# Weight sums, row finishing, output operands and the pool's silu laid at fixed places in a one-core encoder layer

## The chip, the core and the metric

The kernel runs on one core of one Trainium2 chip. The metric is the device time of one execution in microseconds, from the first instruction to the last; lower is better. Five engines matter here: TensorE (PE, matmul), VectorE (DVE), ScalarE (ACT), GpSimd (POOL, nearly idle) and SyncE (SP), which issues almost every DMA.

## The reference

One bidirectional encoder layer, in float32, for 1024 tokens of width 2048:

```python
mod = jax.nn.silu(c) @ w_ada + b_ada
shift, scale, gate = jnp.split(mod, 3, axis=-1)
h = rmsnorm(x, pre_g) * (1.0 + scale[:, None]) + shift[:, None]
proj = h @ w_in
q, k, v, gate_a, u, gate_p = jnp.split(proj, SPLIT_POINTS, axis=-1)
y_a = windowed_gqa(q, k, v, rel_table, sink) * jax.nn.silu(gate_a)
y_p = multiscale_pool(u, w_pool_grp, pool_scale) * jax.nn.silu(gate_p)
g = jax.nn.sigmoid(h @ w_merge + b_merge)
g_a, g_p = jnp.split(g, N_BRANCHES, axis=-1)
merged = g_a * (y_a @ w_br_attn) + g_p * (y_p @ w_br_pool)
o = merged @ w_out
return x + gate[:, None] * rmsnorm(o, post_g)
```

w_in is 2048 x 4608, w_merge 2048 x 4096, w_out 2048 x 2048, the two branch weights 1024 x 2048, w_ada 2048 x 6144. The pool groups average over windows of 2, 4, 8 and 16 tokens.

## The kernel before, in words

**Products.** Every float32 product is made of three matmuls in a rounded float32 form. `split` (L90) takes a tile apart: ACT copies it to the rounded form (hi), DVE subtracts that from the source (lo). PE then adds hi·hi, lo·hi and hi·lo. The large products use a scheme of seven products in place of eight for each 2 x 2 blocks (Strassen and Winograd): `strassen` (L203) makes one "pair" of 256 output columns from seven products of 12 matmuls, each 128x512. The seven need sums of operand blocks (T1 to T4, made once) and of weight blocks (S1 to S4). PE's results lie in three PSUM tiles, X, V and Z; ACT copies them or DVE adds them to earlier parts (u, p, c).

**First pass.** A ramp turns x and makes the first four pairs. `pass1` then runs the pairs 4 to 25, and hands out small steps between products: 36 steps for the modulation (weigh, L458, adds one row of w_ada times silu(c) to `acc` on DVE; sum_columns, L414, adds over partitions with the matmuls PM; mod_columns, L420, writes modc), 32 `gate_step`s (L646, the same for the gate, in `gacc`), the gate's columns, and the 16 `weight_sums` (L617). A weight sum loads four 128x512 blocks of w_out (tag "sw"), makes S1 to S4 in four DVE operations and stores them to DRAM (ws_dS1 to ws_dS4), for the output stage. Its three parts are fetch, make and keep. Before the change they lie from the first step on, evenly over the 22 pairs, and DVE's share of them is placed by the scheduler.

The pairs 26 to 33 run beside the second half of x: fetch_x (L721) loads a tile into the ring `xin` (four buffers), turn_x (L728) transposes it on PE, then modulate and `pre` (L748) prepare operands. Attention follows, then the pool: for each of eight row blocks `window` and `mix` make a window sum, a grouped product and a silu of a loaded gate (tile `sil`, L951).

**Output stage.** The branch products give m in pieces, through DRAM (m_d). `merged_sums` makes operand sums of m (t and B12). `out_pair` (L1145) runs four times, over two halves of the tokens and two of the columns, (0,0), (0,1), (1,0), (1,1); each has seven products of 48 matmuls (`out_mm`, L1110: eight weight blocks, two PSUM tiles, three matmuls). Weights come from w_out or from the stored sums through a ring `wr` of four tiles (512 KB each, two weight blocks) and are split into whi and wlo, four buffers each. `put_step` (L1076) makes one moving operand (mh, ml) out of m, for all four parts at once, after a product, by the hooks after_00 to after_11 (L1279 to L1307).

Rows of o are multiplied by the post norm's weights and squared for the norm. When all four column blocks of a row block are known, `finish_block` (L1132) makes x + o·scale in one DVE operation and stores it. `first_rows` (L1255) does this for the first half's rows during the second half: it loads o from o_d where it isn't kept, and x (tiles `mo`, a ring), two row blocks ahead of the finishing.

**What sets the order.** A tile scheduler places each engine's instructions by priorities and needs, and adds the waits. An instruction that is marked with keep_in_program_order isn't moved: it comes directly behind the instruction that the program wrote ahead of it on the same engine. Each engine, and SP's queue of DMA issues, works in order.

Of the kernel before, what the change touches and what calls it, by code (L numbers as in the profile page):

```python
# [20 lines left out]
P = 128  # L21
# [21 lines left out]
def encoder_layer(ctx: ExitStack, tc: tile.TileContext, x, c, table, w_ada, b_ada, pre_g,  # L43
# [46 lines left out]
    def split(hi, lo, src):  # L90
        nc.scalar.activation(hi, src, AF.Copy)  # L91
        nc.vector.tensor_tensor(lo, src, f32(hi), ALU.subtract)  # L92

    def add(o, a, b, eng=None):
        (eng or nc.vector).tensor_tensor(o, a, b, ALU.add)  # L95

    def sub(o, a, b):
        nc.vector.tensor_tensor(o, a, b, ALU.subtract)
# [488 lines left out]
    wsp = ev_ctx.enter_context(pool("wsum", 6, side="right"))  # L587
# [29 lines left out]
    def weight_sums(j, i):  # L617
# [18 lines left out]
        def keep():  # L636
            for name, t in done:
                store(ws_rows(name)[:, j, i * 512:(i + 1) * 512], t)

        return fetch, make, keep  # L640
# [66 lines left out]
    assert len(steps) == 48 and max(steps) < 7 * n1  # L707
    pass1(n1, side, EASY, steps)
# [39 lines left out]
    def pre(j):  # L748
        t2[j] = pre_op(j, h1, h2, lambda: sp.tile([P, 512], F32, tag="tf", name=uid("tf"), bufs=4))

    side.extend(lambda j=j: pre(j) for j in range(4))
    pass1(PAIRS - i, side, ((0, 1, 2, 4, 5, 6),))
    assert not side
# [154 lines left out]
    with pool("pool") as pp:  # L908
# [30 lines left out]
        def mix(g, j):  # L939
# [9 lines left out]
            sg = pp.tile([P, S], F32, tag="sil", name=f"sil{i}")  # L949
            load(sg, proj_d[COL_GP + i * P:COL_GP + (i + 1) * P, :])  # L950
            nc.scalar.activation(sg, sg, AF.Silu)  # L951
# [11 lines left out]
            store(yp_d[i * P:(i + 1) * P, :], sg)  # L963

        for g, w in enumerate(POOLS):
# [35 lines left out]
    for b, w in enumerate((w_ba, w_bp)):  # L1001
# [4 lines left out]
        else:  # L1006
# [69 lines left out]
    def put_step(n, op, m, t2):  # L1076

        name = MOVING[n]
        for jp in range(JP):
            b11, b12, b21, b22 = (m[kh][jp][:, :, c * 256:(c + 1) * 256] for kh in range(2) for c in range(2))  # L1080
            src = {"B11": b11, "T3": b11, "T2": t2[jp], "B21": b21, "T4": b21, "T1": b12, "B22": b22}[name]
            hi, lo = slot("mh", F32R, (P, 2, 256)), slot("ml", F32R, (P, 2, 256))
            if m is mt and n == 0 and jp == JP - 1:
                tc.keep_in_program_order(nc.scalar.activation(hi, src, AF.Copy))
                sub(lo, src, f32(hi))
            else:
                split(hi, lo, src)
            op[name][jp] = hi, lo
            if name == "B11":
                sub(b11, t2[jp], b11)  # L1090
            elif name == "B21":
                sub(b21, b21, t2[jp])
# [39 lines left out]
    def finish_block(T, n, scale):  # L1132
        r = held.pop((T, n))
        nc.vector.scalar_tensor_tensor(r, r, scale, xrow.pop((T, n)), op0=ALU.mult, op1=ALU.add)
# [10 lines left out]
    def out_pair(half, i, op, after):  # L1145

        final = half == 1 and i == 1
        keep = half == 1 or i == 1
# [15 lines left out]
        def product(wname, mov, pbs, fresh=False):  # L1164

            ws = split_weights(wname)
            nj = 2 * JP
            for j in range(nj - 2):
                w = next(ws)
                for t in range(2):  # L1170
                    out_mm(pbs[t], op, mov, j, t, w, fresh and j == 0, False)
            w = list(ws)
            for t in range(2):
                for j in (nj - 2, nj - 1):
                    out_mm(pbs[t], op, mov, j, t, w[j - nj + 2], False, j == nj - 1)

# [9 lines left out]
        def result(blk, t, src, dst):  # L1186
# [5 lines left out]
            if keep:  # L1192
# [13 lines left out]
        after(0)  # L1206
        product("S3", "T3", bv, True)
        p7 = copies(kept("p7"), bv)
        after(1)
        product("S2", "T2", bz)  # L1210
        u2 = copies(kept("u2"), bz)
        after(2)
# [4 lines left out]
        after(3)  # L1217
# [4 lines left out]
        after(4)  # L1222
# [6 lines left out]
        after(5)  # L1229
        if not final:  # L1230
# [4 lines left out]
            after(6)  # L1235
            return
        c12 = [slot("c12", F32) for _ in range(2)]
# [9 lines left out]
    put_step(0, ops[0], mt, mt2)  # L1247
    put_step(1, ops[0], mt, mt2)
# [30 lines left out]
    def after_00(n):  # L1279
        if n < 5:  # L1280
            put_step(n + 2, ops[0], mt, mt2)
        if n == 6:
            nextm.extend(merged_tiles())
            fetch_merged(nextm, 0)

    def after_01(n):
        if n == 0:
            fetch_merged(nextm, 1)
        if n == 1:
            for jp in range(JP):  # L1290
                merged_sums(nextm, nextt2, jp)
        for step in ((), (), (0,), (1, 2), (3, 4), (5,), (6,))[n]:
            put_step(step, ops[1], nextm, nextt2)

    def after_10(n):
        if n == 0:
            for _ in range(4):
                ring.extend(row_tiles())
# [61 lines left out]
```

## Time and profile before

| what | value |
|---|---|
| median of 3 runs | 2161.96 us (2157.30, 2161.96, 2163.28) |
| profiled execution | 2163.38 us |
| its span in the profile | 2161.6 us |
| mean granted clock of PE | 0.996 |
| DVE's busy time, 150 to 450 us | 226.47 us |
| last stall of PE (Z, first matmul of the last product) | 2141.88 us, 2.64 us |

The profile comes from one execution. The page gives busy times and slices, `--waits`-like lists give for each engine and line what it waited for, and the timeline gives single instructions with their start, their duration and, in brackets, the idle time ahead of them and who ended it. The time between span and device time, 1.8 us, lies around the program. "SPq" is the issue of a DMA, which is not its transfer. The main stages start at about 100 us (first pass), 850 (attention), 1180 (pool), 1517 (branch products) and 1826 (output stage).

### The profile page before, as it was taken

Reading aid. Unit: us, or ns where it says so; the run is one execution under the profiler, and the core shown is the slowest. Engines: PE = TensorE matmul, PEld = TensorE weight load, DVE = VectorE, ACT = ScalarE, POOL = GpSimd, SP = SyncE. Lnnn points to the kernel's source line nnn. Section 1 sums busy time; section 2 is a strip of 40 time slices with the busy share of each in tenths; the row PEclk is TensorE's granted clock in tenths of the full one; section 3 lists DMA queues with packets and bytes.
Section 4 is the critical chain, followed back from the end, with each engine's and each line's share of the span. In section 5 each row is a group of like instructions: output and inputs, shape, how many; then the busy total and the mean of one; then the engine's idle time right before and its main releaser. Section 6 shows DMA issues by size and latency. Waiting matters only on the chain.

```text
span 2161.6 us, 28949 instructions
## 1 busy us (share of the span) xinstructions
PE 2101.6 (97%) x9567; PEld 1716.7 (79%) x9567; DVE 1535.7 (71%) x2754; ACT 1129.2 (52%) x2124; POOL 7.5 (0%) x66
## 2 busy tenths in 40 slices
PE   6999999999999999999999999999999999999997
PEld 3587878888888888888888878888788887878776
DVE  5787777776436676777776878656867878878656
ACT  5653434444374546767775433334645544767554
POOL 0000000000000000000000000000000000000000
PEclk9999999999999999999999999999999999999999
DMA  9888899975443355445445756755654754776986
GB/s 329 287 278 293 293 307 307 323 244 161 151 144 115 117 172 196 164 155 197 155 152 177 250 183 208 245 178 180 221 175 156 239 169 159 264 257 213 301 299 213
DMA packets 303255, 466.11 MB, mean 216 GB/s; under 512 B 23882, under 2 KB 144866, under 8 KB 303104
## 3 DMA queue, kind: packets, MB, share of 16 engines
q1 hardware_dynamic: 301648, 462.02, 65.2%
q0 software_dynamic: 1120, 2.19, 0.3%
q8 instruction: 75, 1.23, 0.2%
q14 instruction: 76, 0.62, 0.1%
q10 hardware_dynamic: 336, 0.06, 0.0%
HBM read 340.41 MB, written 125.85 MB: 216 GB/s over the span
## 4 chain that ended last, share of the span: by engine, by line
PE 75%; DMA 10%; DVE 9%; issue 2%; ACT 2%; SPq 1%; DVEq 0%; ACTq 0%; POOLq 0%
PE Z L228 25%; PE V L228 16%; PE X L228 16%; DVE wlo L92 2%; PE Z L1115 1%; PE Z L1113 1%; PE Z L1114 1%; DMA mo<-in_x_dram 1%; DMA sw<-in_w_out_dram 1%; PE X L1115 1%; PE V L1115 1%; PE V L1113 1%; PE V L1114 1%; PE X L1113 1%; PE X L1114 1%
## 5 line engine op out<-in xcount | busy, mean ns | idle before, releaser
L91 ACT ACTIVATE whi<-raw 128x512 fp32r<-128x512 f32 (+1 forms) x528 | 320.5, 610 | 500.5 <-PE Z L228 256.7
L92 DVE TENSOR_TENSOR wlo<-raw,whi 128x512 fp32r<-128x512 f32 (+1 forms) x528 | 346.6, 662 | 161.4 <-PE Z L228 112.2
L91 ACT ACTIVATE whi<-wr 128x512 fp32r<-128x512 f32 x224 | 138.7, 628 | 92.9 <-DVE wlo L92 30.4
L92 DVE TENSOR_TENSOR wlo<-wr,whi 128x512 fp32r<-128x512 f32 x224 | 149.4, 688 | 43.2 <-ACT whi L91 41.0
L95 DVE TENSOR_TENSOR raw<-raw,raw 128x512 f32<-128x512 f32 x80 | 55.1, 689 | 83.5 <-DMA raw<-in_w_merge_dram 58.5
L1035 ACT ACTIVATE gt<-gt,cols 128x512 f32<-128x512 f32 x64 | 46.0, 723 | 97.9 <-DMA gt<-proj_d 82.1
L228 PE MATMUL V<-T3h,whi 128*128 128x512 f32 x336 | 92.1, 393 | 2.9 <-DVE u L95 2.9
L228 PE MATMUL Z<-B22h,whi 128*128 128x512 f32 x336 | 93.6, 398 | 1.2 <-ACT u L283 1.2
L228 PE MATMUL Z<-T1h,whi 128*128 128x512 f32 x336 | 92.0, 392 | 2.7 <-ACT u L238 1.8
L228 PE MATMUL X<-B11h,whi 128*128 128x512 f32 x336 | 92.5, 393 | 2.1 <-ACT B11h L91 0.8
L228 PE MATMUL V<-T4h,whi 128*128 128x512 f32 x336 | 92.2, 393 | 0.0
L228 PE MATMUL Z<-B22l,whi 128*128 128x512 f32 x336 | 92.1, 394 | 0.0
L228 PE MATMUL Z<-T2h,whi 128*128 128x512 f32 x336 | 91.5, 392 | 0.0
L228 PE MATMUL X<-B11l,whi 128*128 128x512 f32 x336 | 91.3, 390 | 0.2 <-DVE B11l L92 0.2
L228 PE MATMUL Z<-B22h,wlo 128*128 128x512 f32 x336 | 91.3, 392 | 0.0
L228 PE MATMUL Z<-T1l,whi 128*128 128x512 f32 x336 | 91.0, 390 | 0.2 <-DVE T1l L92 0.2
L228 PE MATMUL V<-T3h,wlo 128*128 128x512 f32 x336 | 91.1, 391 | 0.0
L228 PE MATMUL V<-T3l,whi 128*128 128x512 f32 x336 | 91.0, 390 | 0.0
L228 PE MATMUL X<-B21h,whi 128*128 128x512 f32 x336 | 90.9, 390 | 0.0
L228 PE MATMUL V<-T4l,whi 128*128 128x512 f32 x336 | 90.9, 390 | 0.0
L228 PE MATMUL V<-T4h,wlo 128*128 128x512 f32 x336 | 90.8, 389 | 0.0
L228 PE MATMUL Z<-T1h,wlo 128*128 128x512 f32 x336 | 90.7, 390 | 0.0
(308 smaller groups left out, 4851.2 us busy)
## 6 DMA issues: line engine op xcount, KB each, us to landing
part<-part_d SPq DMA_DIRECT2D x136, 256.0 KB, 5.1
ada<-in_w_ada_dram SPq DMA_DIRECT2D x128, 256.0 KB, 5.8
raw<-in_w_in_dram SPq DMA_DIRECT2D x64, 512.0 KB, 4.3
raw<-in_w_merge_dram SPq DMA_DIRECT2D x64, 512.0 KB, 5.3
wr<-ws_dS SPq DMA_DIRECT2D x64, 512.0 KB, 5.1
wr<-in_w_out_dram SPq DMA_DIRECT2D x48, 512.0 KB, 5.3
proj_d<-part SPq DMA_DIRECT2D x68, 256.0 KB, 2.2
sw<-in_w_out_dram SPq DMA_DIRECT2D x64, 256.0 KB, 5.8
```

What stands on the lines that cost most here:

```text
L91: nc.scalar.activation(hi, src, AF.Copy)
L92: nc.vector.tensor_tensor(lo, src, f32(hi), ALU.subtract)
L95: (eng or nc.vector).tensor_tensor(o, a, b, ALU.add)
L228: nc.tensor.matmul(ps, w_[:, i], op[mov][j][m_], start=fresh and i == 0 and n == 0, stop=i == nj - 1 and n == 2, skip_group_check=True)
L1035: nc.scalar.activation(gt, gt, AF.Sigmoid, bias=cols[:, col:col + 1])
L1113: nc.tensor.matmul(pb, hi, w[0], start=first, stop=False, skip_group_check=True)
L1114: nc.tensor.matmul(pb, lo, w[0], start=False, stop=False, skip_group_check=True)
L1115: nc.tensor.matmul(pb, hi, w[1], start=False, stop=last, skip_group_check=True)
```

## The change

1. The weight sums. The four DVE operations of a sum are pinned. Eleven sums are laid from step 70 of the first pass on, behind the 36 modulation steps (which end with about step 70) and among the gate steps; five lie in the pairs 26 to 33, one per pair. They have six buffers in the first part (wsum1) and five in the second (wsum2, also used by `pre`); to make room `xin` has three buffers in place of four.
2. The pool. The gate tile `sil` is loaded one mix ahead, and the silu is pinned on ACT.
3. Operands. `put_step` becomes `put_op(n, jp)`, one part at a time. hi, lo and the follow-up sums of m are pinned, as are both operations of merged_sums. They are laid behind every second weight block of a product (`between`), no longer after it; in the first out_pair each operand is made during the product before the one that uses it.
4. Row finishing. The operation of `finish_block` is pinned, and a step of `first_rows` comes twice per product.

No computation changes, and the number of instructions on each engine stays.

```diff
-            at = [(at, step) for at, step in ((at, steps.get(7 * k + at)) for at in range(7)) if step]
+            at = [(at, step) for at in range(7) for step in steps.get(7 * k + at, ())]
...
-            sub(a["21"], a["11"], a["21"])
-            sub(s2, a["22"], a["21"])
-            add(a["11"], a["11"], s2)
-            sub(a["12"], a["12"], s2)
+            keep(sub(a["21"], a["11"], a["21"]))
+            keep(sub(s2, a["22"], a["21"]))
+            keep(add(a["11"], a["11"], s2))
+            keep(sub(a["12"], a["12"], s2))
...
-    steps = {}
-    for n, three in enumerate(weight_sums(j, h_) for h_ in range(2) for j in range(KT // 2)):
-        for at, step in zip((0, 5, 7), three):
-            steps[7 * n1 * n // 16 + at] = step
-    pass1(n1, side, EASY, steps)
+    def lay_out(n, first, last):
+        steps = {}
+        for k in range(n):
+            for at, step in zip((0, 5, 7), sums.popleft()):
+                steps.setdefault(first + (last - first) * k // n + at, []).append(step)
+        return steps
+    pass1(n1, side, EASY, lay_out(11, 70, 7 * n1 - 2))
...
-    xin = ev_ctx.enter_context(pool("xin", 4, side="right"))
+    xin = ev_ctx.enter_context(pool("xin", 3, side="right"))
+    wsp = mid.enter_context(pool("wsum2", 5))
...
-    pass1(PAIRS - i, side, ((0, 1, 2, 4, 5, 6),))
+    pass1(PAIRS - i, side, ((0, 1, 2, 4, 5, 6),), lay_out(5, 0, 35))
...
-            load(sg, proj_d[COL_GP + i * P:COL_GP + (i + 1) * P, :])
-            nc.scalar.activation(sg, sg, AF.Silu)
+            sg = sils.pop()
+            keep(nc.scalar.activation(sg, sg, AF.Silu))
...
+            if i < NH - 1:
+                fetch_gate_of(i + 1)
...
-                sub(b12, b12, m[0][jp][:, :, 0:256])
+                keep(sub(b12, b12, m[0][jp][:, :, 0:256]))
-                sub(t2[jp], m[1][jp][:, :, 256:512], b12)
+                keep(sub(t2[jp], m[1][jp][:, :, 256:512], b12))
...
-        nc.vector.scalar_tensor_tensor(r, r, scale, xrow.pop((T, n)), op0=ALU.mult, op1=ALU.add)
+        keep(nc.vector.scalar_tensor_tensor(r, r, scale, xrow.pop((T, n)), op0=ALU.mult, op1=ALU.add))
...
                     out_mm(pbs[t], op, mov, j, t, w, fresh and j == 0, False)
+                if j % 2:
+                    between(n, j // 2)
...
+    def between_00(n, jp):
+        if n < 6:
+            put_op(n + 1, jp, ops[0], mt, mt2)
+        if jp == JP - 1 and n == 5:
+            nextm.extend(merged_tiles())
+            fetch_merged(nextm, 0)
+        if jp == JP - 1 and n == 6:
+            fetch_merged(nextm, 1)
...
+    def between_01(n, jp):
+        if n == 1:
+            merged_sums(nextm, nextt2, jp)
+        for k in ((), (), (0,), (1, 2), (3,), (4,), (5,))[n]:
+            put_op(k, jp, ops[1], nextm, nextt2)
...
+    def between_11(n, jp):
+        if jp % 2 and n < 3:
+            steps(1)
```

The first place is DVE at the end of the second group of modulation steps. acc<-ada is a step of the modulation, modc<-PM reads the matmuls that follow the last of them, sw<-sw is part of a weight sum, raw and wlo belong to the running pair. Before:

```order
L463 SCALAR_TENSOR_TENSOR acc_1699<-ada_1970,sc,acc_1699 128x512
L92 TENSOR_TENSOR wlo_2082<-raw_1903,whi_2081 128x512
L95 TENSOR_TENSOR p_466_1869<-p_466_1869,u_489_1991 128x512
L463 SCALAR_TENSOR_TENSOR acc_1699<-ada_2020,sc,acc_1699 128x512
L95 TENSOR_TENSOR sw_2143<-sw_2143,sw_2264 128x512
L463 SCALAR_TENSOR_TENSOR acc_1699<-ada_2020,sc,acc_1699 128x512
L92 TENSOR_TENSOR wlo_2100<-raw_1905,whi_2099 128x512
L421 TENSOR_TENSOR modc<-PM_2025,cols 128x4
```

And now:

```order
L470 SCALAR_TENSOR_TENSOR acc_1691<-ada_1945,sc,acc_1691 128x512
L470 SCALAR_TENSOR_TENSOR acc_1691<-ada_1990,sc,acc_1691 128x512
L102 TENSOR_TENSOR p_461_1852<-p_461_1852,u_480_1966 128x512
L470 SCALAR_TENSOR_TENSOR acc_1691<-ada_1990,sc,acc_1691 128x512
L96 TENSOR_TENSOR wlo_2048<-raw_1878,whi_2047 128x512
L102 TENSOR_TENSOR raw_2039<-raw_2039,raw_2041 128x4x128
L428 TENSOR_TENSOR modc<-PM_1995,cols 128x4
```

The sums are gone from here; the first of the 16 now stands behind the last modc.

The second place is DVE where the branch products end and the output stage begins. c<-Z is the last result of the branches, pv and m are the merged rows, ml is the lo part of the first moving operand, wlo that of the first weights. Before:

```order
L1050 TENSOR_TENSOR p_3413_16829<-p_3413_16829,gt_16784 128x512
L98 TENSOR_TENSOR m_15645<-t_3435_16964,m_15645 128x2x256
L95 TENSOR_TENSOR pv_16937<-pv_16937,p_3413_16829 128x512
L1046 TENSOR_TENSOR c_16957<-Z_16792,gt_16853 128x512
L92 TENSOR_TENSOR ml_16996<-m_15644,mh_16995 128x512
L95 TENSOR_TENSOR pv_16959<-pv_16959,c_16957 128x512
L92 TENSOR_TENSOR ml_17000<-m_15645,mh_16999 128x512
L92 TENSOR_TENSOR wlo_17026<-wr_17013,whi_17025 128x512
```

And now:

```order
L102 TENSOR_TENSOR pv_16941<-pv_16941,p_3413_16833 128x512
L1068 TENSOR_TENSOR c_16961<-Z_16796,gt_16857 128x512
L96 TENSOR_TENSOR wlo_17040<-wr_17027,whi_17039 128x512
L102 TENSOR_TENSOR pv_16963<-pv_16963,c_16961 128x512
L105 TENSOR_TENSOR m_15649<-m_15649 128x2x256
L105 TENSOR_TENSOR t_3435_16968<-m_15653,m_15649 128x512
L96 TENSOR_TENSOR ml_16972<-m_15646,mh_16971 128x512
L105 TENSOR_TENSOR m_15646<-t_3261_16037,m_15646 128x2x256
L96 TENSOR_TENSOR ml_16977<-m_15647,mh_16976 128x512
```

The first ml was made ahead of the last result before; now the last sums of m (m, t) stand ahead of it. On PE two X matmuls stand ahead of the last branch product's 12 (Z<-B22), where four stood.

The third place is SP's queue in the third and fourth out_pair, with the finishing rows: wr are the output stage's weights, mo the ring of finishing tiles, o_d the stored rows of o, x the input. Before:

```order
L1104 DMA wr_19260<-ws_dS_98 128x2x512
L1135 DMA out_dram<-mo_18696 128x512
L1104 DMA wr_19282<-ws_dS_98 128x2x512
L1135 DMA out_dram<-mo_18697 128x512
L1107 DMA wr_19325<-in_w_out_dram 128x2x512
L1264 DMA mo_18696<-o_d 128x512
L1107 DMA wr_19347<-in_w_out_dram 128x2x512
L1139 DMA mo_18696<-in_x_dram 128x512
L1135 DMA out_dram<-mo_18698 128x512
L1107 DMA wr_19369<-in_w_out_dram 128x2x512
L1264 DMA mo_18697<-o_d 128x512
```

And now:

```order
L1153 DMA out_dram<-mo_18697 128x512
L1157 DMA mo_18697<-in_x_dram 128x512
L1122 DMA wr_19276<-ws_dS_98 128x2x512
L1281 DMA mo_18697<-o_d 128x512
L1153 DMA out_dram<-mo_18698 128x512
L1122 DMA wr_19298<-ws_dS_98 128x2x512
L1157 DMA mo_18698<-in_x_dram 128x512
L1281 DMA mo_18698<-o_d 128x512
L1125 DMA wr_19341<-in_w_out_dram 128x2x512
```

Between a tile's store (out<-mo) and the load of o_d into the same tile there were two weight loads; now there is one.

More of the change, by code (lines that the diff above doesn't have):

```diff
@@ L702, in encoder_layer @@
     n1 = -(-2 * len(side) // 7)
[L703 to L708 removed]
+    sums = deque(weight_sums(j, h_) for h_ in range(2) for j in range(KT // 2))
+    def lay_out(n, first, last):
[3 more added lines that the diff above has]
+                steps.setdefault(first + (last - first) * k // n + at, []).append(step)
+        assert max(steps) < last + 2
+        return steps
+    pass1(n1, side, EASY, lay_out(11, 70, 7 * n1 - 2))
     assert not side
@@ L1074, in encoder_layer, with put_op @@
     ssq = const.tile([P, NB, 4], F32, name="ssq_o")
-    def put_step(n, op, m, t2):
+    def put_op(n, jp, op, m, t2):
         name = MOVING[n]
[L1079 to L1092, printed above, removed]
+        b11, b12, b21, b22 = (m[kh][jp][:, :, c * 256:(c + 1) * 256] for kh in range(2) for c in range(2))
+        src = {"B11": b11, "T3": b11, "T2": t2[jp], "B21": b21, "T4": b21, "T1": b12, "B22": b22}[name]
+        hi, lo = slot("mh", F32R, (P, 2, 256)), slot("ml", F32R, (P, 2, 256))
+        split(hi, lo, src, True)
+        op[name][jp] = hi, lo
+        if name == "B11":
+            keep(sub(b11, t2[jp], b11))
+        elif name == "B21":
+            keep(sub(b21, b21, t2[jp]))
     def fetch_merged(m, kh):
@@ L1143, in row_tiles, with out_pair @@
         return m[:, 0], m[:, 1]
-    def out_pair(half, i, op, after):
+    def out_pair(half, i, op, between, after=None):
         final = half == 1 and i == 1
-        keep = half == 1 or i == 1
+        stays = half == 1 or i == 1
+        count = iter(range(7))
         g = {}
@@ L1166, in product @@
             ws = split_weights(wname)
-            nj = 2 * JP
+            n, nj = next(count), 2 * JP
             for j in range(nj - 2):
@@ L1191, in result @@
             nc.vector.tensor_tensor(dst, src, g[nh], ALU.mult)
-            if keep:
+            if stays:
                 held[T, n] = dst
@@ L1246, in encoder_layer @@
     ops = [new_op(JP), new_op(JP)]
-    put_step(0, ops[0], mt, mt2)
-    put_step(1, ops[0], mt, mt2)
+    for jp in range(JP):
+        put_op(0, jp, ops[0], mt, mt2)
     nextm, nextt2 = [], {}
@@ L1310, in after_11 @@
+    def between_11(n, jp):
+        if jp % 2 and n < 3:
+            steps(1)
+        if jp == JP - 1 and n in (2, 4):
             for T in (4, 5) if n == 2 else (6, 7):
```

96 lines of the change are left out of this document (45 added, 51 removed).

## The prediction

> **What bounds the kernel now.** The first view is the page's row of busy time, the second the list of what TensorE (PE) waited for: waiter, line, releaser, then total us, times and the longest.
>
> ```profile
> PE 2101.6 (97%) x9567; PEld 1716.7 (79%) x9567; DVE 1535.7 (71%) x2754; ACT 1129.2 (52%) x2124; POOL 7.5 (0%) x66
> ```
> ```profile
> PE XT L398 <- DVE turn L390: 11.4, 3, 9.6
> PE b L353 <- DMA sink_t<-in_attn_sink_dram: 7.0, 1, 7.0
> PE X L1115 <- DVE wlo L92: 5.7, 2, 3.3
> PE PM L417 <- DVE acc L463: 4.9, 2, 2.5
> PE Z L1115 <- DVE wlo L92: 4.0, 3, 1.7
> PE V L228 <- DVE u L95: 2.9, 3, 1.7
> PE Z L1113 <- ACT u L1183: 2.6, 1, 2.6
> PE Z L228 <- ACT u L238: 1.8, 1, 1.8
> PE V L1115 <- DVE wlo L92: 1.6, 1, 1.6
> PE Z L228 <- ACT u L283: 1.2, 2, 0.9
> ...
> PE X L1113 <- DVE u L95: 0.6, 1, 0.6
> ```
> PE is the bound: busy for 97% of the 2161.6 us span. The change leaves its instruction count alone, so it can return only PE's idle time. The two longest rows belong to the start of the kernel and the row of L1183 to its very end, where order has not moved; those 21.0 us stay. The other rows above add up to 5.7 + 4.9 + 4.0 + 2.9 + 1.8 + 1.6 + 1.2 + 0.6 = 22.7 us, and they are all places that the change touches.
>
> A stall can cost more than its gap. The next view cuts windows of 4 us: two after the PM stalls, one after the longest X stall, one after the other X stall. The column to read is the granted clock, third from the end.
>
> ```profile
> 199.00:203.00 4.00, 4.00 (x12) 3.18 (x11) 2.58 (x5) 0.91 (x2) 0.00 (x0) 0.59 1.01 353
> 304.00:308.00 4.00, 4.00 (x12) 3.15 (x11) 1.91 (x5) 0.63 (x1) 0.00 (x0) 0.59 0.94 291
> 1836.00:1840.00 4.00, 4.00 (x19) 3.29 (x18) 4.00 (x7) 2.35 (x5) 0.00 (x0) 1.00 0.61 155
> 2079.00:2083.00 4.00, 3.67 (x9) 2.92 (x10) 2.77 (x5) 0.63 (x1) 0.00 (x0) 0.58 0.59 172
> ```
> Three of the four have a clock near 0.59, which takes 0.41 x 4 = 1.6 us each, 4.9 us together; the third has none, though its gap was the longest. So up to 22.7 + 4.9 = 27.6 us can go. The third row gives PE's pace as well: 19 matmuls in 4.00 us, 0.21 us each.
>
> The Trainium skill ("TensorE: Matmul & The Clock Gate", Part 1) has the clock fall to half after an idle window of about 3.4 us. This trace disagrees on both sides: the halved stretches follow gaps of 2.4 to 2.5 us, and the one gap of 3.3 us is followed by full clock. By that rule of the Trainium skill the 4.9 us would not belong to the stalls, and would not come back with them.
>
> **Modulation groups.** DVE's timeline before the second PM stall, and PE's row there:
>
> ```profile
> 294.77 0.69 DVE L98 TENSOR_TENSOR sw<-sw,sw 128x512 f32<-128x512 f32 x1 [1.40 <-DMA sw<-in_w_out_dram]
> 295.49 0.69 DVE L95 TENSOR_TENSOR sw<-sw,sw 128x512 f32<-128x512 f32 x1
> 296.10 0.68 DVE L98 TENSOR_TENSOR sw<-sw,sw 128x512 f32<-128x512 f32 x1
> ...
> 301.95 0.74 DVE L463 SCALAR_TENSOR_TENSOR acc<-ada,sc,acc 128x512 f32<-128x512 f32 x1
> ```
> ```profile
> 302.84 1.02 PE L417 MATMUL PM<-ones,acc 128*128 128x1 f32 x8 [2.38 <-DVE acc L463]
> ```
> The weight sums (sw) wait for their loads in DVE's queue, and the accumulation that PM needs stands behind them: 1.40 of waiting and three operations at about 0.60 are 3.2 us, more than the 2.38 us stall. Over the whole kernel:
>
> ```profile
> DVE sw L98 <- DMA sw<-in_w_out_dram: 29.0, 15, 4.5
> ```
> In the changed order no sum stands on DVE before the last of these groups is summed. The 4.9 (PM) and 2.9 (V) us and the two slow stretches (3.2) make 11.0. PM itself moved five matmuls earlier in one group, and u<-V still queues behind accumulations, so I leave 1.0 there: **10.0 back**.
>
> Eleven sums now lie among the gate's accumulation and five among the x steps. Whether waiting sums cost PE there is shown by before itself: the first rows are the sums in 330 to 450 us (one addition each, so seven sums) and DVE's wait for their loads, the last is all that PE waited for in 350 to 560.
>
> ```profile
> L95 DVE TENSOR_TENSOR sw<-sw,sw x7: 682/691/694, 330.2 to 432.3; 128x512 f32<-128x512 f32 x7
> its engine sat idle before it (us, times) until:
>   DMA sw<-in_w_out_dram: 12.7, 5
> ```
> ```profile
> PE V L228 <- DVE u L95: 0.3, 1, 0.3
> ```
> 12.7 us of waiting in DVE cost PE 0.3, because no matmul needs the gate's running sum before the stage ends. Eleven sums at that rate are 0.5 us; I take **0.5 lost** (bounds: 0, and 11 x 2.5 = 28 were each as bad as a PM stall).
>
> The x stage loses one of four xin buffers and gets five sums in SP's queue.
>
> ```profile
> xt<-in_x_dram SPq DMA_DIRECT2D x12, 256.0 KB, 3.4
> ```
> ```profile
> SPq L724 <- PE b L731: 27.1, 12, 5.0
> ```
> The 12 loads of x land in 3.4 us (median) and each already waited for a buffer, 27.1 / 12 = 2.3 us. With three buffers a load can start only when the turn three back is through. By the order some 41 matmuls lie between a turn and the third after it, 8.7 us at 0.21, so the load's 3.4 fits; two of the 12 stand right behind a sum's loads on SP, which wait for stores, and arrive with about 1 us in hand. **1.0 lost** (bounds: 0, and 12 x 3.4 = 41).
>
> **Pool silu.** ACT before the 1.8 us stall of Z:
>
> ```profile
> 1289.08 1.06 ACT L951 ACTIVATE sil<-sil 128x1024 f32<-128x1024 f32 x1 [7.18 <-DVE wlo L92]
> ```
> The silu waits here for its buffer and its load, 7.18 us, and holds all of ACT's queue; the copy of Z that PE waits for (L238) stands behind it. Loading one mix ahead takes the wait away, but the pinned silu keeps a fixed place. The row of L238 (1.8) and the shorter of the two of L283 (0.3) make 2.1; I take **1.3 back** and leave 0.8 for a silu of 1.06 that still meets a copy.
>
> **From the branch to the output stage.** DVE and PE of before:
>
> ```profile
> 1834.60 3.09 DVE L92 TENSOR_TENSOR wlo<-wr,whi 128x512 fp32r<-128x512 f32 x5
> ```
> ```profile
> 1835.34 0.73 PE L1115 MATMUL X<-wlo,mh 128*128 128x512 f32 x2 [3.26 <-DVE wlo L92]
> ```
> Three rows of the PE list meet here: 3.26, 0.9 (L283) and 0.6 (L1113), 4.7 in all. After the change the first ml is pinned behind c<-Z: c, wlo, pv, m, t, ml, six operations at 0.60 (five in 3.09 in the row above) = 3.6 us after Z is there, and 0.4 for the last matmul's end. PE has only two X matmuls for that time, and they stand ahead of Z. So one stall of 4.0 takes the place of three of 4.7; then an ml comes every 1.2 us, and PE needs one in 12 matmuls, 2.5 us. **0.5 back** (bounds: 4.7 back, or 0.9 lost if the 4.0 start a slow stretch).
>
> **Output stage.** DVE at one of its stalls, and what it waited for over the stage:
>
> ```profile
> 1894.41 0.69 DVE L98 TENSOR_TENSOR t<-m,m 128x512 f32<-128x512 f32 x1 [2.35 <-DMA m<-m_d]
> ```
> ```profile
> DVE mo L1134 <- DMA mo<-in_x_dram: 14.2, 6, 4.7
> ```
> Each wait holds the wlo behind it, and PE's stalls on wlo are 5.7 + 4.0 + 1.6 - 3.3 (counted above) = 8.0, plus 1.6 of clock: 9.6. The t<-m now stands some 20 us later, behind weights of the product that is running, so its load (issued around 1897 by the count of rows) is there: 1.7 back. The other 7.9 come from the finishing rows. They are now spread one per half product (24 matmuls, 5 us), x loaded two steps ahead, which is 10 us against:
>
> ```profile
> wr<-in_w_out_dram SPq DMA_DIRECT2D x4, 512.0 KB, 5.3
> out_dram<-mo SPq DMA_DIRECT2D x6, 256.0 KB, 7.4
> mo<-o_d SPq DMA_DIRECT2D x4, 256.0 KB, 5.7
> mo<-in_x_dram SPq DMA_DIRECT2D x4, 256.0 KB, 7.4
> ```
> So x is landed when DVE comes to it. What is late next is SP: four loads of o_d into a buffer wait until that buffer's store is done, and now only one weight load stands between store and load where two stood. A store takes 7.4 us; SP runs four weights (10 us) ahead, lands one in 5.3, and hi and lo take some 1.3 more, so about 3.5 are to spare. The first wait, 7.4 less 2.5 for the weight between, uses that up, and the second puts the next weight 1 to 4 us late. I leave 2.5 there: 7.9 - 2.5 = 5.4, with the 1.7 **7.1 back** (bounds: 9.6 back; 2.4 lost, if each of the four weights is late by 3).
>
> **Sum.** 10.0 - 0.5 - 1.0 + 1.3 + 0.5 + 7.1 = 17.4. The profiled execution took 2163.4 us (span 2161.6 and 1.8 around it), so **2146**. That execution lies 1.4 above the median of the runs, 2161.96.
>
> **Rivals.**
> - *The finishing rows keep their stalls.* The store-before-load chain on SP makes all four weights late, and pins keep DVE from running ahead of a row whose x is late. For it: the 7.4 us store against 2.5 us of product per weight. Against: the x loads themselves are 10 us ahead. Of the 7.9 nothing comes back: 2146 + 5.4 = **2151**.
> - *Slow stretches remain.* The 4.0 us stall at the branch's end starts one (1.6), and two of the three found above were not the stalls' doing (2 x 1.6): 2146 + 4.9 = **2151**. Against: both stretches begin right behind their stalls, and the clock stayed at 1.00 after 3.26 us. The window of 3.4 us that the Trainium skill gives (same page and part) would end here.
> - *Slower: x loads behind sums.* In the x stage every load waits for its buffer, then 3.4 us for landing, while SP stands on a sum's load that waits for its store; PE waits at every transpose. Price 3.4 each, 12 x 3.4 = 41: less the 1.0 counted, 2146 + 40 = **2186**. It decides from six late turns (20 us, all the gain). Against: three turns make 8.7 us.
> - *Nothing moved in time.* The sums find as many waits among the gate's steps, and the pins as many in the output stage: the gain stays under 6, **2160**. Against: the 0.3 us row above.
>
> **Chances.** Forecast 0.50, finishing rows 0.18, slow stretches 0.08, nothing 0.14, slower 0.10. The forecast's own range is 2135 (all 27.6 gone) to 2153. The range of 8 in 10 runs from 2135 to 2163: it takes in both middle rivals and most of "nothing". A measurement of this kernel can tell about 0.3% from no change, 6.5 us: faster (under 2155.5) has 0.50 + 0.18 + 0.08 = 0.76, same 0.14, slower 0.10.
>
> **What would show it.** In the profile of after: no PM and no V row on L228's sums in PE's waits, clock near 1.00 at 150 to 350; sw waits in DVE still some 25 us, but PE's below 1 in 300 to 560. At 1828 one stall of about 4 us, X behind ml. No mo row above 3 us among DVE's waits; a wait of SP for out_dram<-mo near 2040 to 2060, and one or two stalls on wlo behind it. The forecast is wrong if XT or x rows of over 3 us show in 540 to 690, or if the mo rows keep their 14.2.

## The result, and the profile after

The changed kernel takes 2157.66 us (median of 17 runs, 2153.73 to 2164.74) against 2161.82 us of before (17 runs beside it). The ratio is **0.9982, 95% interval 0.9972 to 0.9993**: 4 us faster, where the forecast was 16. The time lies in the range of 8 in 10 (2135 to 2163) and outside the forecast's own (2135 to 2153); the gain is a quarter of what was forecast, and it is what the rival "nothing moved in time" gave (under 6 us).

The profiled execution of after took 2153.73 us (span 2152.0), the fastest of its 17, that of before 2163.38, above its median. So the two traces differ by 9.6 us and the medians by 4.2. The table shows where. For each stretch it adds up the distances between the starts of successive matmuls, less PE's pace of 0.227 us per 512 columns: what PE lost there, gaps and slow clock together. It compares one profile with one; how far other profiles of the same code scatter stands behind the experiments.

| stretch of before (us) | before | after | difference |
|---|---|---|---|
| ramp, 0 to 150 | 33.0 | 31.7 | -1.3, not touched |
| modulation, 150 to 350 | 13.1 | 2.3 | -10.9 |
| gate, 350 to 560 | 3.2 | 8.2 | +5.0 |
| x stage, 560 to 700 | 5.4 | 8.4 | +3.0 |
| 700 to 1250 | 19.2 | 16.2 | -3.0, not touched |
| pool, 1250 to 1420 | 4.1 | 5.6 | +1.5 |
| branch products, 1420 to 1815 | 3.3 | 4.4 | +1.1 |
| branch's end, 1815 to 1846 | 5.6 | 7.3 | +1.7 |
| rest of the output stage | 14.8 | 8.1 | -6.7 |

The stretches that nothing touched hold 4.3 of the 9.6, so the touched ones return 5.3, which agrees with the medians. In them 17.6 us were gained and 12.3 lost again, in this pair of profiles.

What PE waited for after (waiter, line, releaser, then total us, times, longest):

```profile
PE V L235 <- DVE u L102: 6.2, 3, 3.3
PE X L1132 <- DVE ml L96: 3.9, 1, 3.9
PE b L745 <- ACT xt L739: 3.5, 2, 2.0
PE X L1131 <- ACT whi L95: 2.9, 1, 2.9
PE Z L1131 <- ACT u L1206: 2.2, 1, 2.2
PE X L235 <- DVE part L102: 1.9, 1, 1.9
```
The rows of PM on DVE's accumulation and of wlo on the output stage are gone; no sum waits in front of either. In their place stand V in the gate stretch (two of the three, 3.3 and 1.5), the x tiles, one stall at the branch's end, weights of the output stage, and the pool. The windows of after over modulation, gate and x stage:

```profile
150.00:350.00 200.00, 199.91 (x898) 165.44 (x897) 135.32 (x216) 82.23 (x134) 0.00 (x0) 1.00 0.61 204
450.00:560.00 110.00, 105.17 (x470) 85.48 (x469) 74.07 (x106) 43.17 (x71) 2.28 (x3) 1.00 0.84 279
560.00:700.00 140.00, 136.49 (x636) 112.42 (x635) 81.04 (x130) 77.64 (x176) 0.00 (x0) 1.00 0.66 214
```
PE is now busy for 199.91 of the 200 us of the first window. In the same windows of before:

```profile
150.00:350.00 200.00, 192.55 (x844) 158.08 (x843) 150.92 (x244) 78.74 (x129) 0.00 (x0) 0.98 0.90 299
450.00:560.00 110.00, 110.00 (x487) 89.97 (x486) 64.33 (x87) 48.11 (x80) 2.28 (x3) 1.00 0.59 185
560.00:700.00 140.00, 140.00 (x662) 116.06 (x661) 70.37 (x111) 76.71 (x174) 0.00 (x0) 1.00 0.43 134
```
The traffic (last two columns, DMA share and GB/s) moved from the first stretch into the other two, and PE's idle time went with it.

**The gate stretch.** DVE, then SP, ahead of the stall of 3.3 us at 503.99:

```profile
495.47 0.68 DVE L105 TENSOR_TENSOR sw<-sw,sw 128x512 f32<-128x512 f32 x1
501.31 0.69 DVE L105 TENSOR_TENSOR ws<-raw 128x512 f32<-128x512 f32 x1 [5.16 <-DMA raw<-in_w_merge_dram]
501.92 0.68 DVE L105 TENSOR_TENSOR sw<-sw,sw 128x512 f32<-128x512 f32 x1
502.64 0.69 DVE L102 TENSOR_TENSOR sw<-sw,sw 128x512 f32<-128x512 f32 x1
503.25 0.68 DVE L102 TENSOR_TENSOR u<-V,u 128x512 f32<-128x512 f32 x1
```
```profile
493.65 0.38 SPq L187 DMA_DIRECT2D raw<-in_w_merge_dram  x1
...
496.18 0.33 SPq L645 DMA_DIRECT2D ws_dS<-sw  x1
496.56 1.15 SPq L633 DMA_DIRECT2D sw<-in_w_out_dram  x1
502.63 1.04 SPq L645 DMA_DIRECT2D ws_dS<-sw  x2
```
DVE does not wait for a sum's load: in after that wait is nil (29.0 us before). It waits for `raw`, the running pair's own weights, and then makes two operations of a pinned sum (501.92 and 502.64); u, which frees V for PE, stands behind both. At the other stall (524.85, 1.53 us) two sum operations stand between ws and u as well. Between 400 and 560 us these are the only two pairs where that is so, and at 442 us a wait for raw of 5.1 us passed without a stall of PE. Had u followed ws directly, at 501.92 and 522.79, it would have begun 1.33 us sooner each time: by that estimate 2.7 of the 4.8 us are the sums on DVE, and the rest the late raw.

The load of raw was issued at 493.65, 4.2 us before the pair's first matmul. From pair to pair that lead shrinks: 9.6, 9.4, 9.1, 6.9, 6.5, 4.8, 4.2, 2.7 us for the eight pairs up to 520 us, where before kept 7 to 10. SP falls behind by up to 2 us a pair, and PE stalls only at the end of the stretch. The load at 493.65 itself waited 2.7 us for a wlo of DVE, and DVE had waited for the raw before it, so the lag goes round. What SP waited for in 450 to 700 us:

```profile
SPq L738 <- PE b L745: 26.2, 8, 5.0
...
SPq L187 <- DVE wlo L96: 18.1, 12, 5.3
SPq L645 <- DVE sw L105: 16.8, 17, 4.8
...
SPq L633 <- DMA ws_dS<-sw: 13.4, 6, 9.0
```
The stores of sums (L645) wait for DVE, and loads of the next sum (L633) can wait until those stores are done, because a sum takes five of the six (or five) buffers and the next one's loads stand some 7 steps behind, at the step of the store. The pairs' weights and the x tiles are loaded from the same queue. But the waits of L633 are not what the four stalls hang on: 9.0 of the 13.4 us are one wait near 557, which no stall of PE follows, and 2.1 fall before 540. That stores wait for DVE's sums isn't new either: in 350 to 540 us SP waited 16.3 us for sw before and 19.6 after.

**The x stage.** ACT at the first of the two stalls:

```profile
615.90 0.72 ACT L739 ACTIVATE xt<-xt,rstd 128x512 f32<-128x512 f32 x1 [2.57 <-DMA xt<-in_x_dram]
```
The load of this x tile was issued at 610.53, directly behind four stores and four loads of sums, 7.6 us after the load of x ahead of it:

```profile
602.93 0.33 SPq L738 DMA_DIRECT2D xt<-in_x_dram  x1
603.35 0.38 SPq L311 DMA_DIRECT2D part_d<-u  x1
603.83 3.09 SPq L645 DMA_DIRECT2D ws_dS<-sw  x4
608.18 0.32 SPq L311 DMA_DIRECT2D part_d<-p  x1
608.55 1.93 SPq L633 DMA_DIRECT2D sw<-in_w_out_dram  x4
610.53 0.90 SPq L738 DMA_DIRECT2D xt<-in_x_dram  x2
```
The four loads of the sum waited for no store here, and x did not wait for its buffer. About 2.8 of the 7.6 us are waits of SP for DVE, the rest is the issue of the ten transfers, one after the other. The tile was there at 615.9, 5.4 us later, where the two ahead of it had taken 3.1 and 3.3. Ahead of the second stall stands the same block (626.44 to 634.95).

**The branch's end.** PE and DVE:

```profile
1828.06 0.80 PE L1132 MATMUL X<-whi,ml 128*128 128x512 f32 x1 [3.92 <-DVE ml L96]
```
```profile
1824.18 0.69 DVE L1068 TENSOR_TENSOR c<-Z,gt 128x512 f32<-128x512 f32 x1
...
1827.32 0.69 DVE L96 TENSOR_TENSOR ml<-m,mh 128x512 fp32r<-128x512 f32 x1
```
It is the chain of six operations that was forecast, with one stall of 3.92. The clock behind it, in a window of 4 us, and the same behind the pool's stall of 1.85 and the gate's of 3.30 (granted clock third from the end):

```profile
504.00:508.00 4.00, 4.00 (x18) 3.30 (x19) 4.00 (x5) 1.23 (x2) 0.00 (x0) 1.00 0.90 271
...
1829.00:1833.00 4.00, 4.00 (x11) 3.05 (x10) 3.96 (x8) 2.31 (x5) 0.00 (x0) 0.50 0.61 225
1331.00:1335.00 4.00, 4.00 (x12) 3.15 (x11) 4.00 (x21) 1.54 (x2) 0.00 (x0) 0.60 0.64 235
```

**The pool.** ACT's wait for the gate tile, of after:

```profile
ACT sil L964 <- DMA sil<-proj_d: 22.9, 6, 8.9
```
Before it was 26.8 us in 6 waits. The load made one mix ahead still comes late; the tile has one buffer, and the store of the tile in it has to be done first.

### The profile page after: what moved, and what is told of

Same layout as the page of the kernel before. It is cut to its first block, busy times and chain, and to the rows that moved or that the text cites. A ratio compares the mean times of both kernels' runs of the same rounds, so it can differ in the third digit from the quotient of the medians.

```text
span 2152.0 us, 28951 instructions
## 1 busy us (share of the span) xinstructions
PE 2098.7 (98%) x9567; PEld 1716.3 (80%) x9567; DVE 1539.9 (72%) x2754; ACT 1129.6 (52%) x2124; POOL 7.4 (0%) x66
## 4 chain that ended last, share of the span: by engine, by line
PE 84%; DMA 8%; DVE 4%; ACT 2%; issue 1%; SPq 1%; DVEq 0%; ACTq 0%
PE Z L235 28%; PE X L235 18%; PE V L235 18%; DMA raw<-in_w_merge_dram 3%; PE Z L1131 2%; PE Z L1132 2%; PE Z L1133 2%; PE V L1131 1%; PE V L1133 1%; PE V L1132 1%; PE X L1132 1%; PE X L1133 1%; PE X L1131 1%; DVE wlo L96 1%; DMA xt<-in_x_dram 1%
## 5 line engine op out<-in xcount | busy, mean ns | idle before, releaser
L235 PE MATMUL X<-B11h,wlo 128*128 128x512 f32 x336 | 91.5, 392 | 0.0
L235 PE MATMUL Z<-T2l,whi 128*128 128x512 f32 x336 | 90.7, 390 | 0.0
```

The source lines that it names most:

```text
L235: nc.tensor.matmul(ps, w_[:, i], op[mov][j][m_], start=fresh and i == 0 and n == 0, stop=i == nj - 1 and n == 2, skip_group_check=True)
```

## The experiments

Theory: the three groups of edits each work where they were aimed, and three side effects take most of it back: SP's queue stands at the sums' stores and loads (gate stretch, x stage), the pins put the first lo part behind six operations (branch's end), and the gate tile's single buffer undoes the early load (pool). Rivals: the losses are chance of one profile; DVE's fuller queue or the DMA engines' load sets them. All ratios are to the kernel before, on the same chip, with 95% intervals. The change itself was not run again beside the experiments, so a difference between one of their ratios and its 0.9982 compares two series of runs.

**Sums alone.** The kernel before with part 1 of the change:

```diff
+    pass1(n1, side, EASY, lay_out(11, 70, 7 * n1 - 2))
...
+    xin = ev_ctx.enter_context(pool("xin", 3, side="right"))
...
+    pass1(PAIRS - i, side, ((0, 1, 2, 4, 5, 6),), lay_out(5, 0, 35))
```


> The kernel before with the weight sums' new places alone (11 behind the modulation groups, 5 in the x stage, three xin buffers), and nothing else of the change. In the two profiles the sums' part gave back 10.9 us at 150 to 350 us and lost 6.4 at 450 to 560 and 3.0 at 560 to 700. Theory 1 (the gain of the modulation groups is given back where the sums now lie, because SP's queue brings the pairs' weights late): about -1.5 us against before, ratio 0.999, PE stalls V<-u of 1 to 3 us near 504 and 525 and two waits for xt near 617 and 641. Theory 2 (the losses are chance of one profiled run): -9 us or better, ratio 0.996 or less, and no such stalls.

Measured: 0.9977 (0.9966 to 0.9987), 5 us faster: between the two theories' figures. PE in 150 to 700 us:

```profile
PE b L745 <- ACT xt L739: 3.6, 2, 2.5
PE V L235 <- DVE u L102: 2.8, 2, 1.9
```
The same four stalls at the same four places (502, 523, 616, 641 us): they are not chance, and they belong to the sums. The stretch from 150 to 700 lost 21.8 us before and 18.7 here, a net gain of 3.1, so the ratio is a little better than the trace.

**Output stage alone.** The kernel before with parts 3 and 4:

```diff
-        split(hi, lo, src)
+        split(hi, lo, src, True)
...
+                if j % 2:
+                    between(n, j // 2)
...
+        keep(nc.vector.scalar_tensor_tensor(r, r, scale, xrow.pop((T, n)), op0=ALU.mult, op1=ALU.add))
```


> The kernel before with the output stage's part alone (operands and sums of m pinned between the weights, finishing rows pinned every half product). Theory 1: the rest of the output stage gives back 6 to 7 us, the branch's end loses 1 to 2 (one stall of 4 us and a slow stretch after it in place of three stalls), so -4 to -6 us, ratio 0.997 to 0.998. Theory 2 (the output stage's finishing rows still wait, SP stands before loads of o_d): 0 us, ratio 1.000.

Measured: 0.9979 (0.9965 to 0.9992), 4.5 us faster, as theory 1 had it. The five wlo stalls of the output pairs are gone; 3.9 us of X behind ml at the branch's end and 3.8 us of X behind whi at 1912 stand in the list.

**Pool alone.** The kernel before with part 2:

```diff
-            sg = pp.tile([P, S], F32, tag="sil", name=f"sil{i}")
-            load(sg, proj_d[COL_GP + i * P:COL_GP + (i + 1) * P, :])
-            nc.scalar.activation(sg, sg, AF.Silu)
+            sg = sils.pop()
+            keep(nc.scalar.activation(sg, sg, AF.Silu))
```


> The kernel before with the pool's part alone (gate loaded one mix ahead, silu pinned). Theory 1: the gate tile has one buffer, so the load made earlier in the program still waits for the store of the tile before it; ACT still waits about 23 us for it (26.8 in before), and the time is within 2 us of before, ratio 0.999 to 1.001. Theory 2 (what I predicted): -1.3 us or better and no wait of ACT for the gate's load above 2 us.

Measured: 0.9991 (0.9977 to 1.0005): no difference that this can tell. ACT still waits 25.2 us for the gate tile's load, as theory 1 had it. The three parts alone add up to 0.9947, and the whole change has 0.9982; that gap of 0.0035 is more than the some 0.0025 that the four intervals allow, and I can't explain it.

**Sums' transfers on another queue.**

```diff
-                load(a[name], wo_rows(kh)[:, j, n0:n0 + 512])
+                nc.gpsimd.dma_start(a[name], wo_rows(kh)[:, j, n0:n0 + 512])
...
-                store(ws_rows(name)[:, j, i * 512:(i + 1) * 512], t)
+                nc.gpsimd.dma_start(ws_rows(name)[:, j, i * 512:(i + 1) * 512], t)
```


> The changed kernel with all loads and stores of the weight sums issued by POOL (GpSimd), which is nearly idle, instead of SP. If SP's order makes the pairs' weights and the x tiles late (theory 1), the stalls near 504, 525, 617 and 641 us go and 6 to 9 us come back: ratio to before 0.994 to 0.996. If it is the DMA engines' load (theory 2) or DVE's queue (theory 3), the stalls stay and the time is that of the changed kernel, ratio 0.998.

Measured: 1.0171 (1.0150 to 1.0193), 37 us slower than before: none of the theories. PE from 350 to 750 us:

```profile
PE b L745 <- ACT xt L739: 13.7, 4, 6.0
PE V L235 <- DVE u L102: 9.5, 4, 7.3
PE b L745 <- ACT h L748: 6.4, 3, 5.1
PE b L668 <- issue: 4.6, 1, 4.6
```
From 560 to 750 us the sums' loads took 7.4 us to land (4.6 in the change, 560 to 700), and those of x, still on SP, 7.4 (4.5 in the change, 3.4 before). It doesn't tell the theories apart, since it brought a cost of its own.

**Sums stored sooner**, on SP as in the change:

```diff
-            for at, step in zip((0, 5, 7), sums.popleft()):
+            for at, step in zip((0, 4, 5), sums.popleft()):
```


> The changed kernel with each weight sum made one step and stored two steps earlier (steps 0, 4, 5 in place of 0, 5, 7), so that a store is issued some 5 us ahead of the next sum's loads, which use its buffers. Theory 1 (SP stands at loads that wait for stores, 11.3 us in the x stage, and falls behind by about 1 us a pair in the gate stretch): the waits of SP for stores of sums fall below 4 us, the stalls near 617 and 641 us go, those near 504 and 525 are half or less, 4 to 8 us back: ratio 0.994 to 0.9965. Theory 2 (DVE's pinned sums or the number of transfers set it): the stalls stay, ratio 0.998.

Measured: **0.9941 (0.9925 to 0.9956)**, 9 us below the change (5 to 13). PE in 450 to 700 us waited for one thing:

```profile
PE b L745 <- ACT h L748: 1.2, 1, 1.2
```
The gate stretch and the x stage lost 9.0 us in place of 16.7. Three things moved. SP's wait of L633 for stores of sums is down to 0.4 us in the x stage (540 to 700), where the change has 11.3 of its 13.4; but the late x tiles had not hung on it, and in 350 to 540 us it is 4.6 here against 3.5. In SP's queue the loads of x now stand in between a sum's stores and loads (604.40, 610.29, 612.98, 616.64), and raw is issued 9.0, 9.2, 7.9, 7.7 and 5.6 us ahead of its pair from 432 to 512, where the change has 6.9 falling to 2.7. And on DVE u now follows ws directly at the pairs near 500 and 520:

```profile
497.50 0.69 DVE L105 TENSOR_TENSOR ws<-raw 128x512 f32<-128x512 f32 x1 [1.27 <-DMA raw<-in_w_merge_dram]
498.11 0.68 DVE L102 TENSOR_TENSOR u<-V,u 128x512 f32<-128x512 f32 x1
```
The DMA engines' load alone is not the cause: the number of transfers is the same, the engines are as busy (0.87 in 450 to 560, 0.84 in the change), and raw takes as long to land (6.8 and 6.4 us at the median, 430 to 530). For the x stage theory 1 stands, as the block of stores and loads that SP issues ahead of x, and not as a wait for buffers. In the gate stretch this run moves SP's stores and DVE's sums together, so it doesn't separate theory 1 from DVE's queue; the trace of the change shows both at work.

**First operand not pinned.**

```diff
-        split(hi, lo, src, True)
+        first = m is mt and n == 0
+        if first:
+            ins = nc.scalar.activation(hi, src, AF.Copy)
+            if jp == JP - 1:
+                keep(ins)
+            sub(lo, src, f32(hi))
+        else:
+            split(hi, lo, src, True)
...
-            keep(sub(b11, t2[jp], b11))
+            ins = sub(b11, t2[jp], b11)
+            if not first:
+                keep(ins)
```


> The changed kernel, with the first operand of the output stage (the lo parts of B11 and the sums that follow them) not pinned, as before the change. If the pins make the 3.9 us stall of X behind ml near 1828 us and the slow stretch behind it, ml of the first three parts stands ahead of the branch's last result again, the stall is under 2 us and 3 to 5 us come back: ratio to before 0.996 to 0.997. If the last result of Z and the chain behind it set that time in any order, the stall stays above 3 us and the ratio is 0.998.

Measured: **0.9945 (0.9928 to 0.9962)**, 8 us below the change, more than expected. PE's stalls at the branch's end:

```profile
1821.81 1.21 PE L235 MATMUL Z<-B22h,whi 128*128 128x512 f32 x4 [1.08 <-ACT u L290]
1830.16 0.50 PE L1142 MATMUL X<-wlo,mh 128*128 128x512 f32 x1 [0.31 <-DVE wlo L96]
```
3.92 fell to 0.31, and the stretch from 1815 to 1846 loses 2.3 us in place of 7.3. These 5.0 are inside the interval of the measured difference (4 to 12 us, from the two ratios' intervals).

**Two buffers for the gate tile.**

```diff
-            sg = sils.pop()
+            sg = sils.pop(0)
...
-            sils.append(pp.tile([P, S], F32, tag="sil", name=f"sil{i}"))
-            load(sils[0], proj_d[COL_GP + i * P:COL_GP + (i + 1) * P, :])
+            sils.append(pp.tile([P, S], F32, tag="sil", name=f"sil{i}", bufs=2))
+            load(sils[-1], proj_d[COL_GP + i * P:COL_GP + (i + 1) * P, :])
```


> The changed kernel with two buffers for the pool's gate tile. If the load made ahead waits for the store of the one buffer, ACT's wait for the gate falls from 22.9 us to under 5, the stall of X behind part near 1331 us goes, and 2 to 4 us come back: ratio 0.996 to 0.9975. If the stalls of the pool have another cause, ACT's wait goes and the ratio stays at 0.998.

Measured: 0.9957 (0.9940 to 0.9973), 5 us below the change. ACT's waits for the gate tile are now

```profile
ACT sil L964 <- issue: 3.1, 1, 3.1
```
none of them a DMA, and PE waits for nothing from 1200 to 1420 us: the stretch from 1250 loses 0.2 us in place of 5.6.

**Merged tiles loaded a little later.**

```diff
-        if jp == JP - 1 and n == 6:
-            fetch_merged(nextm, 1)
+        if n == 0 and jp == 0:
+            fetch_merged(nextm, 1)
```
(the second in the hook of the second out_pair.)

> The changed kernel with the loads of the second eight merged tiles issued a product's quarter into the second out_pair, as before the change, and no longer behind the last product of the first. If SP's queue there (eight loads of m and the stores of p that wait for DVE, ahead of the next weights) makes the 2.9 us stall of X near 1910 us, it goes and about 3 us come back: ratio 0.9965 to 0.9975. If the weights are late for the DMA engines' load alone, the stall stays or moves by a product, ratio 0.998.

Measured: 0.9968 (0.9955 to 0.9981); its interval overlaps that of the change. The stall of 2.9 near 1910 us became two of 1.3 and 1.8. Inconclusive on the time, and against the theory for the trace. That a run whose trace gains nothing there has 0.9968 is also a warning: it and the three runs before it were made on one chip, the other six on another, so up to some 3 us of the 9, 8 and 5 us "below the change" may not belong to the edits.

**The three repairs together:** sums stored sooner, first operand not pinned, two buffers for the gate tile.

> The changed kernel with three edits together: the first output operand not pinned, two buffers for the pool's gate tile, weight sums made and stored sooner. Alone they measured 0.9945, 0.9957 and 0.9941 against before, where the change has 0.9982: 0.0037, 0.0025 and 0.0041 less. Theory 1 (three separate causes, each of which gave back a part of the change's gain): they add, ratio 0.988, 0.985 to 0.990. Theory 2 (they share one cause, such as SP's lag, or the single figures hold chance): ratio 0.991 to 0.994.

Measured: **0.9901 (0.9879 to 0.9922), 2139.43 us**, 20 us below before and 18 below the change. That lies between the two theories' ranges, and its interval reaches into both: of the 0.0103 that the three gave singly, 0.0081 came together. In the profile the three places lose as little as they did singly (table below), which speaks for separate causes. PE's four longest waits behind the ramp:

```profile
PE Z L1140 <- ACT u L1215: 3.2, 1, 3.2
PE X L1140 <- ACT whi L95: 2.4, 1, 2.4
PE b L745 <- ACT h L748: 1.5, 2, 1.1
PE Z L235 <- ACT u L290: 1.3, 2, 1.1
```
The first is the stall ahead of the last product, as before.

**The merged tiles' loads spread.** The same kernel, with

```diff
-        if jp == JP - 1 and n == 6:
-            fetch_merged(nextm, 1)
+        if n == 6:
+            fetch_merged(nextm, 1, (jp,))
```


> The kernel of the three edits, and with them the loads of the second eight merged tiles spread over the last product of the first out_pair, two behind each weight pair, in place of all behind its end. If the stall of X behind whi near 1905 us (2.4 to 3.9 us in every run with the new output stage) comes from SP standing at the stores of p with loads of m on both sides of them, it falls below 1.5 us and the time is 1 to 3 us under that of the three edits. If the stores of p alone set it, the stall stays within 0.5 us.

Measured: 0.9909 (0.9885 to 0.9933), 2141.19 us: no gain over the three repairs. The stall of 2.4 became 1.4 and 0.9, with a new one of 1.2 ahead of it. Of the queue's content there, the stores of p, which wait for DVE, were not moved; whether they set this stall stays open.

**The same stretches in the other profiles.** Counted as in the table above, between the same matmuls by their number (one of fewer than 128 columns counts as 128; this comes within 0.7 us of that table), without the run on the POOL queue:

| stretch | as before there | as in the change there | mended there |
|---|---|---|---|
| modulation | 11.0 to 13.2 (3 profiles) | 1.6 to 2.0 (8) | |
| gate and x stage | 8.0, 9.1, 10.4 | 16.2 to 18.3 (5) | 8.9, 9.1, 10.0 |
| pool | 3.9, 4.0, 4.2 | 1.2, 3.1, 3.5, 4.2, 5.5 | 0.1, 0.1, 0.5 |
| branch's end | 5.6, 6.0, 7.0 | 6.3 to 7.6 (5) | 2.3, 2.4, 2.5 |
| rest of the output stage | 11.1, 14.6, 16.4 | 7.9, 8.3, 11.1, 11.5, 13.1, 13.3 | |

(The last row ends with the last matmul, and leaves out the two runs that moved the merged tiles' loads.) The gain in the modulation, the loss in gate and x stage and what the three edits return stand outside the scatter. The pool's 1.5 lost, the branch end's 1.7 lost and the output stage's full 6.7 don't: on the means the pool and the branch's end moved by 0.5 us, and the output stage returned some 3 us (14.0 to 10.9).

## Why the prediction was wrong, point by point

- **Modulation groups: right.** "10.0 back" came as 10.9, with the slow stretches gone (granted clock 0.98 to 1.00 over 150 to 350 us), and in every profile with the new places. One reading was off: the prediction holds the gap of 3.26 us against the idle window of about 3.4 us that it cites, but that gap is shorter than the window; only the halved clock behind gaps of 2.4 to 2.5 us speaks against it.
- **Gate stretch: the step that failed first.** It said that before itself shows that sums among the gate steps cost nothing, "12.7 us of waiting in DVE cost PE 0.3", and took "0.5 lost". It cost 5.0. The row was of another case: sums that float and wait for their loads. After, DVE waits for no sum's load (29.0 us to 0), and two other things cost. At two pairs two pinned sum operations stand between ws and u and hold V for 1.3 us each; and raw comes late, because SP issues it ever closer to its pair (9.6 to 2.7 us). I had priced what a sum waits for, and neither where a pinned sum stands ahead of u nor how far SP is ahead. Making and storing the sums sooner undid both and returned 7.7 us here and in the x stage; how much each of the two cost is known only by the estimate above (2.7 of 4.8).
- **x stage: right place, wrong size.** "1.0 lost" for two x tiles behind a sum's loads: there were exactly two stalls, 1.5 and 2.0, and 3.0 lost. "About 1 us in hand" was not there: the block of a sum's stores and loads kept SP from x for 7.6 us, and the tile then took 5.4 us to land where the prediction has 3.4. That the sum's loads wait for their stores did not happen at these two. It is the rival "slower" at two turns instead of twelve. (The pace of 0.21 us counts matmuls that the window cuts; starts are 0.227 apart, so 41 matmuls are 9.3 us and not 8.7, which changes little.)
- **Pool: failed.** "Loading one mix ahead takes the wait away": the gate tile has one buffer, so the load can't start before the store of the tile in it is done. ACT waited 22.9 us in place of 26.8, and the forecast 1.3 back did not come: 1.5 lost in this profile, 0.5 back on the mean of five. The buffer count stood in the code. With two buffers the forecast's mechanism works.
- **Branch's end: right stall, wrong sum.** The forecast chain of six operations and the stall of 4.0 came as 3.92. "0.5 back" left out the slow stretch behind the stall, which the prediction names as the worse bound (0.9 lost) and which came (0.50); 1.7 were lost in this profile, 0.5 on the means. The chain could also be left away altogether, which returned 5.0 in the trace.
- **Output stage: right mechanism, a term too large.** No stall of PE on wlo is left, x is ahead of DVE, and no mo row in DVE's waits is above 1 us. SP did stand before the loads of o_d (11.9 us in four waits), and the only stall of PE behind that is one of 0.8, where I had left 2.5. But "7.1 back", which came as 6.7 in this profile, is some 3 on the means, so the agreement is luck in part. What I had not seen is the stall of X behind whi, near 1910 us, behind loads of m and stores of p: 2.4 to 3.8 us in all six profiles with this output stage in the table. Its cause is open.
- **The sum.** Of 17.4 forecast, the two gains were put at 17.1; this pair of profiles has 17.6, the means some 14. The other stretches, forecast together as 0.3 back, lost 12.3 in this pair, and some 8 on the means, all of it in gate and x stage. So the sums' new places were priced at 1.5 and cost about 8, and the output stage's term was too large by about 4. The rival "nothing moved in time" had the size, with a chance of 0.14, but for another reason in the output stage, where the pins did work. The rival of slow stretches was right for the branch's end and wrong for the others.

## What to carry to other kernels

A pin that keeps an operation from floating also fixes what stands behind it: here two sum operations, 1.3 us together, ahead of the one that PE waited for. And transfers laid at one step stand in the queue as a block: here four stores and four loads kept SP from the next load for 7.6 us. So look, for each engine and each queue, at what the pinned work stands ahead of, and check the number of buffers before an earlier load is booked as a gain. Loads whose lead shrinks a little from pair to pair (9.6 to 2.7 us here) show a queue that falls behind well before any engine stalls. And before a term is called right, look at a second profile: the same output stage lost 7.9 us in one and 13.3 in another.

## What the runs showed of the hardware that was not expected

- The stretches of half clock do not go by the length of the gap: 1.85 us (pool) and 3.92 us (branch's end) were followed by 0.60 and 0.50 over 4 us, 3.30 us (gate) by 1.00. With the gaps of before (2.4 and 2.5 with, 3.26 without) no length separates the two kinds.
- With the sums' transfers issued by POOL in place of SP, these took longer in the x stage, and so did those of SP's queue: the sums' loads 7.4 us in place of 4.6, the x tiles 7.4 in place of 4.5. The kernel took 37 us more than before.
